# A fused QKV projection on one core: loads of x two pairs ahead issued in front of two pairs' stores, and two stores of the last pair on the other queue

## The chip, the core and the metric

The kernel runs on one core of a Trainium2 chip. TensorE (PE) multiplies, VectorE (DVE), ScalarE (ACT) and GpSimd (POOL) move and combine data, SyncE (SP) only issues DMAs. PE's weight loads have a row of their own, PEld. The metric is the device time of one execution, in microseconds (us). Three runs of the kernel before gave 360.57, 360.79 and 361.13 us; the median is 360.79 us.

## The reference

```python
def reference(x, w_qkv):               # x (16, 512, 768), w_qkv (768, 2304), float32
    qkv = np.matmul(x, w_qkv)
    q, k, v = qkv[..., :768], qkv[..., 768:1536], qkv[..., 1536:]
    return np.stack([q, k, v], axis=0).astype(np.float32)
```

x is 8192 rows of 768 numbers, 25 MB; the output is 8192 rows of 2304 numbers, 75 MB; the weights are 7 MB.

## The kernel before, in words

**Tiling.** The 8192 rows are worked on in 32 pairs of row blocks; a pair is 2 x 128 rows, numbered 0 to 31 in the code and in this document. (The fourth and fifth pairs are pairs 3 and 4.) The 2304 output columns are two blocks of 1024, called a (q = 0) and b (q = 1) here, and a remainder of 256 between them. "5a" is block a of pair 5.

**Seven products.** From pair 2 on, a pair times a block of 1024 columns is a 2 x 2 by 2 x 2 product computed with seven products in place of eight (a Strassen scheme). Each product is three matmuls of 128x128 by 128x512 that accumulate in one PSUM bank. Products 1 and 2 use bf16 copies of x (`xb`) and of the weights, products 3 to 7 use sums of quarters of x (`sr`, made by `sums_x` on POOL) and of the weights. `do(u, n)` (L269) issues product n of block u and the instructions that carry the bank into the output tile `u.o`: ACT writes a quarter of it (L267 for product 1, L286 for product 6, L292 for product 7, L296 for product 4), DVE adds a bank to a quarter (L293 after L292, L299 after product 3). `summed(a, b)` (L353) runs products 6, 6, 5, 7, 5, 7, 4, 3, 4, 3 of two blocks, 30 matmuls, and then stores each block. Several products share a bank: product 3 accumulates into the bank of product 5 after L293 has read it, product 7 into that of product 6 after L286 has read it.

**x.** `load_x(p, eng)` (L141) loads a pair as four DMAs of 192 KB into a tile `xin` (three buffers): two are issued by SP, two by the queue named. `transpose(p)` (L155) turns it on DVE into `xf`, whole or in two halves; `round_x` (L205) on POOL makes the bf16 copy, `sums_x` (L225 to L229) on POOL the sums.

**Stages.** Pairs 0 and 1 use ordinary bf16 products while the weights arrive. Block a of pair 2 is done among them; its block b (`u2`) is done together with pair 3. Then `two(a, b, early)` (L335) runs pair 3 and pair 4: products 1, the remainder (`rem`, L321), products 2, then `summed`. `early` is a function called in the middle: it transposes the next pair and issues loads. From pair 5 on a loop takes two pairs at a time (`summed` for one, then `plain`, then `summed` for the other); its first pass transposes the first half of pair 6 ahead of pair 5's `summed` and the second half within it. `last` (L412) does pair 31 and stores it in pieces.

**What sets the order.** The schedule is written by hand: each engine and each queue runs its instructions in the order in which the program gives them. SP issues every DMA of this part of the run, loads and stores, in one queue; from pair 9 on, half of every second pair's loads are issued by ACT. A store waits on SP until the last quarter of its half block is written, and everything behind it on SP waits too. Eight semaphores tell of DMAs' landings in turn, and an issue also waits until the DMA that last used its semaphore has landed, so at most eight are in flight.

**Buffers.** Output tiles `o` come from a pool of five and are taken in turn: 5a takes the one of block b of pair 1, 5b that of 3a, the blocks of pair 6 those of 3b and 4a, and 7a that of 4b. The first write to a tile waits until its former contents have been stored. `rem` has two output tiles `orem` of its own.

**Loads around the change.** Pair 5 is loaded in the first `early` (L624 to L626), within pair 3's `two`. In the second `early`, within pair 4's `two`, come the loads of pair 6; the loads of pair 7 come after that `two`:

```python
    def early():
        ahead(ND + 3, True)
        load_x(ND + 4, nc.sync)

    two(quad(ND + 2, 0), quad(ND + 2, 1), early)
    load_x(ND + 5, nc.sync)
    transpose(ND + 4, 2, 0)
```

ND is 2. So SP's order is: stores of `u2`, stores of pair 3 (L306, L307 for a, L310, L311 for b), loads of pair 6, the remainder's store of pair 4 (L331), stores of pair 4, loads of pair 7, loads of pair 8.

**The end.** In `last`, `store_cols` (L391) stores a quarter of a block: one DMA of 256 KB (L397), or two of 128 KB where the quarter crosses a border between two of the three outputs. In the last loop each block's quarter of product 4 is stored from ACT's queue and the quarter of product 3 from SP's; for block b the former is two DMAs. Behind them ACT copies the last remainder (L407) and stores it (L409).

Of the kernel before, what the change touches and what calls it, by code (L numbers as in the profile page):

```python
# [10 lines left out]
def kernel(  # L11
# [20 lines left out]
    nc = tc.nc  # L32
# [10 lines left out]
    CB = 512  # L43
# [81 lines left out]
    def load_x_half(p, h, eng):  # L125
        rows = x_flat[p * 2 * P:(p + 1) * 2 * P, :].rearrange("(g b) k -> b g k", b=G)
        for i in (2 * h, 2 * h + 1):
            eng.dma_start(xin[p][i * G:(i + 1) * G], rows[:, :, i * KC:(i + 1) * KC])
# [12 lines left out]
    def load_x(p, other):  # L141
        xin[p] = xin_pool.tile([P, 2 * P // G, KC], fp32, name="xin")
        load_x_half(p, 0, nc.sync)
        if other is not None:
            load_x_half(p, 1, other)

    def transpose(p, parts=1, which=None):
        if p not in xf:
            xf[p] = xf_pool.tile([P, KT, 2 * P], fp32, name="xf")
        turned = xf[p][:].rearrange("p j (g b) -> p g j b", b=G)  # L150
        rows = xin[p][:].rearrange("p g (a j) -> p g j a", a=G)
        n = 2 * P // G // parts
        for i in range(parts) if which is None else (which, ):
            g = i * n
            nc.vector.transpose(turned[:, g:g + n], rows[:, g:g + n])  # L155
# [84 lines left out]
    def quad(p, q, pool=o_pool, tag="o"):  # L240
        u = Quad()
        u.p, u.q = p, q
        u.o = pool.tile([P, 2, 2 * CB], fp32, name="o", tag=tag)
        u.x = u.y = u.z = None
        return u

    def product(u, n, ps, start):
        t1, t2, t3, t4 = ts[u.q]
        if n <= 2:
            h = (n - 1) * KH  # L250
            lhs = [xb[u.p][:, h + j, :P] for j in range(KH)]
            rhs = [b1[u.q][:, h + j, :] for j in range(KH)]
        else:
            k, t = {3: (4, b22[u.q][:]), 4: (0, t4), 5: (1, t1), 6: (2, t2), 7: (3, t3)}[n]
            lhs = [sr[u.p][:, k, j, :] for j in range(KH)]
            rhs = [t[:, j, :] for j in range(KH)]
        for j in range(KH):
            nc.tensor.matmul(  # L258
                ps[:], lhs[j], rhs[j],
                start=(start and j == 0), stop=(j == KH - 1), skip_group_check=True,  # L260
            )

    def bank():
        return ps_pool.tile([P, CB], fp32, name="ps")

    def evacuate(u):
        nc.scalar.activation(u.o[:, 0, :CB], u.x[:], ident)  # L267

    def do(u, n, out=True):  # L269
        c11, c12 = u.o[:, 0, :CB], u.o[:, 0, CB:]  # L270
        c21, c22 = u.o[:, 1, :CB], u.o[:, 1, CB:]
        if n == 1:
            u.x = bank()
            product(u, 1, u.x, True)
            if out:
                evacuate(u)
        elif n == 2:
            u.z = bank()
            product(u, 2, u.z, True)
            nc.vector.tensor_tensor(c11, c11, u.z[:], op=add)  # L280
        elif n == 6:
            first = u.x is None
            if first:
                u.x = bank()
            product(u, 6, u.x, first)
            nc.scalar.activation(c12, u.x[:], ident)  # L286
        elif n == 5:
            u.y = bank()
            product(u, 5, u.y, True)
        elif n == 7:  # L290
            product(u, 7, u.x, False)
            nc.scalar.activation(c22, u.x[:], ident)  # L292
            nc.vector.tensor_tensor(c22, c22, u.y[:], op=add)  # L293
        elif n == 4:
            product(u, 4, u.x, False)
            nc.scalar.activation(c21, u.x[:], ident)  # L296
        elif n == 3:
            product(u, 3, u.y, False)
            nc.vector.tensor_tensor(c12, c12, u.y[:], op=add)  # L299
# [4 lines left out]
    def store_quad(u):  # L304
        if u.q == 0:
            nc.sync.dma_start(rows_of(0, u.p, 0, H), u.o[:, :, :H])  # L306
            nc.sync.dma_start(rows_of(1, u.p, 0, 2 * CB - H), u.o[:, :, H:])  # L307
        else:
            part = 2 * H - Q_OFF[1]
            nc.sync.dma_start(rows_of(1, u.p, H - part, H), u.o[:, :, :part])  # L310
            nc.sync.dma_start(rows_of(2, u.p, 0, H), u.o[:, :, part:])  # L311
# [9 lines left out]
    def rem(p, eng=nc.sync, between=None):  # L321
        ps = ps_pool.tile([P, 2, REM], fp32, name="ps")
        rem_row(p, 0, ps[:, 0, :])
        if between is not None:
            between()
        rem_row(p, 1, ps[:, 1, :])

        def copied():
            o = or_pool.tile([P, 2, REM], fp32, name="orem")
            act.activation(o[:], ps[:], ident)  # L330
            return lambda: eng.dma_start(rows_of(1, p, R_OFF - H, R_OFF - H + REM), o[:])  # L331

        return copied

    def two(a, b, early, u=None):  # L335

        do(a, 1)
        do(b, 1, u is None)
        if u is None:
            early()  # L340
            rem(a.p)()()
        else:
            middle(u)
            copied = rem(a.p, between=lambda: third(u))
            evacuate(b)
            early()
            copied()()
            fourth(u)
        do(a, 2)
        do(b, 2)  # L350
        summed(a, b)

    def summed(a, b, between={}, store=True):  # L353

        for i, (u, n) in enumerate(
            ((a, 6), (b, 6), (a, 5), (a, 7), (b, 5), (b, 7), (a, 4), (a, 3), (b, 4), (b, 3))
        ):
            do(u, n)
            if n == 3 and store:
                store_quad(u)  # L360
            between.get(i, lambda: None)()
# [28 lines left out]
    def store_cols(u, r, lo, hi, eng):  # L390

        c = Q_OFF[u.q] + lo
        end = Q_OFF[u.q] + hi
        while c < end:
            n = min(end, (c // H + 1) * H)
            row = (2 * u.p + r) * P
            eng.dma_start(  # L397
                out_flat[c // H, row:row + P, c % H:c % H + n - c],
                u.o[:, r, c - Q_OFF[u.q]:n - Q_OFF[u.q]],
            )  # L400
            c = n

    def rem_stored(p, r):
        ps = bank()
        rem_row(p, r, ps[:, :REM])
        o = or_pool.tile([P, 2, REM], fp32, name="orem")
        nc.scalar.activation(o[:, 0, :], ps[:, :REM], ident)  # L407
        row = (2 * p + r) * P
        nc.scalar.dma_start(out_flat[1, row:row + P, R_OFF - H:R_OFF - H + REM], o[:, 0, :])  # L409

    def last(a, b):

        do(a, 1)
        do(b, 1)
        rem_stored(a.p, 0)
        for u in (a, b):
            do(u, 2)
            store_cols(u, 0, 0, CB, nc.sync)
        do(a, 6)
        do(b, 6)  # L420
        for u in (a, b):
            do(u, 5)
            do(u, 7)
            store_cols(u, 1, CB, 2 * CB, nc.sync)
        for u in (a, b):
            do(u, 4)
            store_cols(u, 1, 0, CB, nc.scalar)
            do(u, 3)
            store_cols(u, 0, CB, 2 * CB, nc.sync)
        rem_stored(a.p, 1)  # L430


    ND = 2
# [60 lines left out]
    def middle(u):  # L494
        do(u, 6)
        do(u, 5)
        act.activation(u.o[:, 1, CB:], u.y[:], ident)

    def third(u):
        c22 = u.o[:, 1, CB:]  # L500
        product(u, 7, u.x, False)
        dve.tensor_tensor(c22, c22, u.x[:], op=add)
        do(u, 3)

    def fourth(u):
        do(u, 4)
        store_quad(u)

    def ahead(p, reversed_pair):
        transpose(p)  # L510
        if reversed_pair:
            sums_x(p)
            round_x(p)
        else:
            round_x(p)
            sums_x(p)
# [46 lines left out]
    u = quad(2, 0)  # L563
# [59 lines left out]
    def early():  # L623
        ahead(ND + 2, False)  # L624
        load_x(ND + 3, nc.sync)

    two(quad(ND + 1, 0), quad(ND + 1, 1), early, u2)

    def early():
        ahead(ND + 3, True)  # L630
        load_x(ND + 4, nc.sync)

    two(quad(ND + 2, 0), quad(ND + 2, 1), early)
    load_x(ND + 5, nc.sync)
    transpose(ND + 4, 2, 0)

    for p in range(ND + 3, NP - 1, 2):
# [14 lines left out]
        a, b = quad(p, 0), quad(p, 1)  # L652
        summed(a, b, {5: turned} if first else {}, False)
        c, d = quad(p + 1, 0), quad(p + 1, 1)
        plain(a, b, c, d, early, lambda: rem(c.p)()())
        summed(c, d, {0: lambda: p + 3 < NP and transpose(p + 3, 2, 0)})
    last(quad(NP - 1, 0), quad(NP - 1, 1))


# [28 lines left out]
```

## Time and profile before

| | |
|---|---|
| median of three runs | 360.79 us |
| profiled execution | 360.87 us |
| its span | 359.1 us |
| PE busy | 352.8 us, 98% of the span |
| DVE busy | 262.9 us, 73% |
| ACT busy | 185.5 us, 52% |
| POOL busy | 177.6 us, 49% |
| DMA | 108.10 MB, 301 GB/s on average |

The profile is one execution, read on the core's engines. A row of the timeline has its start, its length in us, engine, line, operation, output<-inputs, and how often it came; in square brackets stands how long the engine was idle before it and what it was waiting for. "SPq" and "ACTq" are the queues' own instructions, such as the issue of a DMA. A row of the DMA view has the tiles, the issuing queue, the number of issues, the size of one and the median time from issue to landing. The chain of work that ended last follows the end of the run back from each step to what released it; its rows are start, length and what. Ends of matmuls are modelled.

### The profile page before, as it was taken

To read this page: it belongs to the slowest core of one execution; us is meant where nothing else is said; L and a number is where in the kernel's file an instruction comes from. 1 tells how busy PE (TensorE), PEld (TensorE's weight loads), DVE (VectorE), ACT (ScalarE), POOL (GpSimd) and SP (SyncE) were. 2 spreads that over 40 slices of the span, in tenths; PEclk is the share of its full clock that TensorE was granted. 3 is DMA by queue.
4 is the path that set the end of the run, shared out by engine and by line. 5 is a ranking of instruction groups with operands and counts; after the bars stand their busy time and mean duration, and the time that the engine had idled before them with its cause. 6 is when DMAs were issued, how large, how long until landed. Compare 5 with 4: busy or idle time off the path is not lost.

```text
span 359.1 us, 5325 instructions
## 1 busy us (share of the span) xinstructions
PE 352.8 (98%) x1776; PEld 252.3 (70%) x1776; DVE 262.9 (73%) x308; ACT 185.5 (52%) x317; POOL 177.6 (49%) x184
## 2 busy tenths in 40 slices
PE   8999999899999999999999999999999999999995
PEld 4474677668777686777868777686877768677674
DVE  3798876696776958778696876959777695877643
ACT  4587755445454554545545454553645545364553
POOL 0031783375666354665535566353665535566420
PEclk9999999999999999999999999999999999999999
DMA  7997999998999898997979899698999989896497
GB/s 298 378 347 236 322 381 382 373 256 328 310 308 348 231 377 208 342 287 241 379 201 381 237 319 325 197 406 216 349 266 306 330 218 373 222 339 235 170 358 263
DMA packets 81563, 108.10 MB, mean 301 GB/s; under 512 B 4992, under 2 KB 61568, under 8 KB 81536
## 3 DMA queue, kind: packets, MB, share of 16 engines
q1 hardware_dynamic: 74288, 102.25, 84.7%
q10 hardware_dynamic: 7248, 5.51, 5.7%
q8 instruction: 14, 0.23, 0.3%
q14 instruction: 13, 0.11, 0.1%
HBM read 32.24 MB, written 75.50 MB: 300 GB/s over the span
## 4 chain that ended last, share of the span: by engine, by line
PE 94%; DMA 3%; ACT 1%; DVE 0%; ACTq 0%; issue 0%; SPq 0%
PE ps L258 77%; PE ps L316 12%; PE ps L479 6%; DMA xin<-in_x_dram 2%; DMA out_dram<-o 2%; ACT xc L166 0%; PE ps L185 0%; ACTq L397 0%; DVE o L299 0%; DVE o L293 0%; ACT o L296 0%; SPq L162 0%; ACT orem L407 0%; SPq L306 0%; ACTq L407 0%
## 5 line engine op out<-in xcount | busy, mean ns | idle before, releaser
L258 PE MATMUL ps<-t,s 128*128 128x512 f32 x720 | 177.9, 395 | 0.0
L258 PEld LDWEIGHTS ps<-t,s 128*128 128x128 f32 x720 | 134.9, 188 | 29.6 <-ACT o L267 0.2
L155 DVE STREAM_TRANSPOSE xf<-xin 128x768 f32<-128x768 f32 (+1 forms) x45 | 93.4, 2077 | 5.6 <-DMA xin<-in_x_dram 5.5
L258 PE MATMUL ps<-b,xb 128*128 128x512 bf16 x360 | 85.4, 379 | 0.0
L293 DVE TENSOR_TENSOR o<-o,ps 128x512 f32<-128x512 f32 x58 | 39.7, 687 | 53.9 <-ACT o L292 53.9
L205 POOL CAST xb<-xf 128x1536 bf16<-128x1536 f32 x28 | 41.2, 1471 | 58.1 <-DVE xf L155 58.1
L225 POOL TENSOR_TENSOR s<-xf 128x384 fp32r<-128x384 f32 x29 | 29.5, 1017 | 72.6 <-DVE xf L155 72.6
L258 PEld LDWEIGHTS <-xb 128*128 128x128 bf16 x360 | 33.9, 98 | 36.8 <-issue 4.2
L292 ACT ACTIVATE o<-ps 128x512 f32<-128x512 f32 x58 | 34.7, 598 | 43.5 <-PE ps L258 43.5
L299 DVE TENSOR_TENSOR o<-o,ps 128x512 f32<-128x512 f32 x60 | 41.1, 687 | 20.0 <-PE ps L258 18.8
L258 PE MATMUL ps<-b,s 128*128 128x512 f32 x180 | 50.7, 390 | 1.1 <-DVE o L293 1.1
L296 ACT ACTIVATE o<-ps 128x512 f32<-128x512 f32 x60 | 35.9, 598 | 25.9 <-PE ps L258 23.4
L369 DVE TENSOR_TENSOR o<-o,ps 128x512 f32<-128x512 f32 x78 | 47.8, 682 | 0.0
L316 PE MATMUL ps<-w_rem,xb 128*128 128x256 bf16 x384 | 47.3, 273 | 0.0
L286 ACT ACTIVATE o<-ps 128x512 f32<-128x512 f32 x60 | 36.0, 601 | 19.5 <-PE ps L258 15.8
L316 PEld LDWEIGHTS <-xb 128*128 128x128 bf16 x384 | 37.2, 98 | 11.6 <-issue 0.8
L330 ACT ACTIVATE orem<-ps 128x512 f32<-128x512 f32 x31 | 18.5, 598 | 48.7 <-PE ps L316 33.4
L258 PEld LDWEIGHTS ps<-b,s 128*128 128x128 f32 x180 | 33.7, 188 | 8.5 <-issue 1.5
L226 POOL TENSOR_TENSOR s<-s,xf 128x384 fp32r<-128x384 f32 x29 | 29.6, 1020 | 2.3
L227 POOL TENSOR_TENSOR s<-xf 128x384 fp32r<-128x384 f32 x29 | 29.4, 1014 | 0.0
L229 POOL TENSOR_TENSOR s<-xf,s 128x384 fp32r<-128x384 f32 x29 | 29.3, 1009 | 0.0
L373 ACT ACTIVATE o<-ps 128x512 f32<-128x512 f32 x26 | 15.6, 599 | 17.4 <-PE ps L258 16.8
(46 smaller groups left out, 160.8 us busy)
## 6 DMA issues: line engine op xcount, KB each, us to landing
out_dram<-o SPq DMA_DIRECT2D x62, 768.0 KB, 4.6
xin<-in_x_dram SPq DMA_DIRECT2D x88, 192.0 KB, 5.6
out_dram<-o SPq DMA_DIRECT2D x65, 256.0 KB, 3.8
out_dram<-orem SPq DMA_DIRECT2D x31, 256.0 KB, 2.4
xin<-in_x_dram ACTq DMA_DIRECT2D x24, 192.0 KB, 4.3
st<-in_w_qkv_dram SPq DMA_DIRECT2D x5, 768.0 KB, 8.0
xin<-in_x_dram SPq DMA_DIRECT2D x2, 768.0 KB, 4.9
st<-in_w_qkv_dram SPq DMA_DIRECT2D x6, 256.0 KB, 6.0
```

Of the source, the lines that this page charges most:

```text
L155: nc.vector.transpose(turned[:, g:g + n], rows[:, g:g + n])
L205: nc.gpsimd.tensor_copy(out=xb[p][:], in_=xf[p][:])
L225: 1: lambda g: g.tensor_tensor(s[:, 1], a21, a22, op=add),
L226: 2: lambda g: g.tensor_tensor(s[:, 2], s[:, 1], a11, op=sub),
L258: nc.tensor.matmul(ps[:], lhs[j], rhs[j], start=(start and j == 0), stop=(j == KH - 1), skip_group_check=True,)
L286: nc.scalar.activation(c12, u.x[:], ident)
L292: nc.scalar.activation(c22, u.x[:], ident)
L293: nc.vector.tensor_tensor(c22, c22, u.y[:], op=add)
L296: nc.scalar.activation(c21, u.x[:], ident)
L299: nc.vector.tensor_tensor(c12, c12, u.y[:], op=add)
L316: nc.tensor.matmul(ps, xb[p][:, j, r * P:(r + 1) * P], w_rem[j // KH][:, j % KH, :], start=(j == 0), stop=(j == KT - 1), skip_group_check= ...
L369: dve.tensor_tensor(c, c, u.z[:], op=add)
```

## The change

The load of x of pair 6 moves out of the second `early` into the first `two` (the branch with `u2`, which runs only for pair 3), right behind `fourth(u)`, which stores `u2`; so it stands on SP ahead of the stores of pair 3. The load of pair 7 moves from behind the second `two` into its `early`; so it stands ahead of the remainder's store and of the stores of pair 4. In `last`, the quarter of product 4 of block b is stored from SP's queue, that of block a from ACT's as before.

```diff
@@ two
             early()
             copied()()
             fourth(u)
+            load_x(a.p + 3, nc.sync)
         do(a, 2)
         do(b, 2)
         summed(a, b)
@@ last
         for u in (a, b):
             do(u, 4)
-            store_cols(u, 1, 0, CB, nc.scalar)
+            store_cols(u, 1, 0, CB, nc.scalar if u is a else nc.sync)
             do(u, 3)
             store_cols(u, 0, CB, 2 * CB, nc.sync)
@@ pairs 3 and 4
     def early():
         ahead(ND + 3, True)
-        load_x(ND + 4, nc.sync)
+        load_x(ND + 5, nc.sync)
 
     two(quad(ND + 2, 0), quad(ND + 2, 1), early)
-    load_x(ND + 5, nc.sync)
     transpose(ND + 4, 2, 0)
```

The number and size of all DMAs and the orders of PE, DVE and POOL are the same before and after; SP issues two DMAs more and ACT two less.

## The prediction

> **What bounds the kernel now.** I read the page's shares first, then the chain of work that ended last, then the timeline around the one place where that chain leaves TensorE, and at last the landings of the DMAs there. The chain by engine, from the page:
>
> ```profile
> PE 94%; DMA 3%; ACT 1%; DVE 0%; ACTq 0%; issue 0%; SPq 0%
> ```
>
> The kernel is bound by TensorE: nearly all of its end is matmuls standing one behind the other. So an edit pays only where TensorE waits, or in the tail behind its last matmul. In order of time the chain leaves TensorE in mid-run once:
>
> ```profile
> 63.85 5.55 DMA out_dram<-o
> 69.45 0.66 DVE o L293
> ```
>
> The reader should not take the first row at its word: the L293 add behind it waits for old stores whose semaphores later DMAs share, and the profile names the last of these. The timeline of all engines shows what stood in front of L293. "T6.0" and "T6.1" below are the two half transposes of pair 6 (pairs count from 0), "5a" and "5b" the two blocks of pair 5:
>
> ```profile
> 62.22 0.84 PE L258 MATMUL ps<-b,s 128*128 128x512 f32 x3
> ...
> 62.90 0.84 PE L258 MATMUL ps<-t,s 128*128 128x512 f32 x3
> ...
> 64.26 4.92 PE L258 MATMUL ps<-t,s 128*128 128x512 f32 x21
> ...
> 64.46 0.69 DVE L299 TENSOR_TENSOR o<-o,ps 128x512 f32<-128x512 f32 x1 [0.67 <-PE ps L258]
> ...
> 65.19 1.28 ACT L286 ACTIVATE o<-ps 128x512 f32<-128x512 f32 x2 [0.81 <-PE ps L258]
> ...
> 67.18 0.60 ACT L292 ACTIVATE o<-ps 128x512 f32<-128x512 f32 x1 [0.71 <-PE ps L258]
> 67.94 1.59 DVE L155 STREAM_TRANSPOSE xf<-xin 128x768 f32<-128x768 f32 x1 [2.79 <-DMA xin<-in_x_dram]
> 68.54 0.60 ACT L292 ACTIVATE o<-ps 128x512 f32<-128x512 f32 x1 [0.76 <-PE ps L258]
> ...
> 69.45 1.25 DVE L293 TENSOR_TENSOR o<-o,ps 128x512 f32<-128x512 f32 x2
> ...
> 70.25 0.94 PE L258 MATMUL ps<-b,s 128*128 128x512 f32 x3 [1.07 <-DVE o L293]
> 70.61 1.63 DVE L155 STREAM_TRANSPOSE xf<-xin 128x768 f32<-128x768 f32 x1
> ...
> 72.38 1.47 POOL L205 CAST xb<-xf 128x1536 bf16<-128x1536 f32 x1 [6.68 <-DVE xf L155]
> ...
> 72.42 1.47 PE L258 MATMUL ps<-b,xb 128*128 128x512 bf16 x6
> ...
> 75.03 1.46 PE L258 MATMUL ps<-b,xb 128*128 128x512 bf16 x6
> ```
>
> VectorE ends L299 at 65.15, then stands 2.79 us at T6.0 because x of pair 6 has not landed; the two L293 adds, whose input was there at 67.78 (67.18 + 0.60), queue behind T6.0 until 69.45. Product 3 of 5a accumulates into the bank that the first L293 reads, so TensorE stops 1.07 us and resumes at 70.25. A late load of x is the only stop of TensorE here.
>
> **The change, step by step.** Edit one: the four DMAs that load x of pair 6 move ahead of the four stores of pair 3, and those of pair 7 ahead of those of pair 4. Nothing is added or removed; 4 loads and 4 stores trade places on SP's queue, twice. SP's issues before:
>
> ```profile
> 51.88 0.50 SPq L311 DMA_DIRECT2D out_dram<-o  x1
> ...
> 53.64 0.37 SPq L306 DMA_DIRECT2D out_dram<-o  x1
> ...
> 54.50 0.69 SPq L307 DMA_DIRECT2D out_dram<-o  x1
> ...
> 55.28 1.05 SPq L310 DMA_DIRECT2D out_dram<-o  x1
> ...
> 56.42 1.10 SPq L311 DMA_DIRECT2D out_dram<-o  x1
> ...
> 57.58 3.50 SPq L128 DMA_DIRECT2D xin<-in_x_dram  x4
> ```
>
> What matters is when the loads land. From narrow windows of the DMA view, the time from issue to landing of the stores issued at 51.88, 53.64, 54.50 and 56.42, then SP's row of the fourth load and its landing:
>
> ```profile
> out_dram<-o SPq DMA_DIRECT2D x1, 768.0 KB, 7.6
> ...
> out_dram<-o SPq DMA_DIRECT2D x1, 768.0 KB, 7.8
> ...
> out_dram<-o SPq DMA_DIRECT2D x1, 256.0 KB, 7.6
> ...
> out_dram<-o SPq DMA_DIRECT2D x1, 768.0 KB, 8.4
> ...
> 60.52 0.57 SPq L128 DMA_DIRECT2D xin<-in_x_dram  x1
> ...
> xin<-in_x_dram SPq DMA_DIRECT2D x1, 192.0 KB, 7.3
> ```
>
> Landings: 59.5, 61.4, 62.1, 64.8 and 67.8. They come in the order of issue and at steps that follow the bytes: 2.0 us for a 768 KB store, 0.7 for 256 KB, 3.0 for the four loads together (64.8 to 67.8). Between 51 and 68 the transfers are a line at a counter, some 7 us long, and a place in the line is a time. Estimate for after, from these steps: the loads of pair 6 take the issue slots from 53.64 on and land at 59.5 + 3.0 = 62.5; the stores of 3a follow at 62.5 + 2.0 + 0.7 = 65.2, those of 3b at 65.2 + 0.7 + 2.0 = 67.9, the loads of pair 7 at 70.9.
>
> T6.0 can then start as soon as L299 ends, at 65.19; its data, there since 62.5, has 2.7 us to spare. It ends at 66.8; the first L293 starts with its ACT input at 67.8 and ends at 68.5. TensorE's rate there is 0.68 us for three matmuls (62.22 to 62.90), 0.227 each, so after 21 of them it comes to product 3 of 5a at 64.26 + 4.77 = 69.03: 0.5 us after L293 is done. The second L293 (input 68.54 + 0.60 = 69.14) ends at 69.85; its product is due at 64.26 + 27 x 0.227 = 70.39, again 0.5 later. So no wait is left. The 30 matmuls of pair 5's ten products took 72.42 - 64.26 = 8.16 us and take 30 x 0.227 = 6.81: **minus 1.35 us**. That is the stop of 1.07 plus what the restart lost before and after it.
>
> What hid the moved stores, and is late next: the stores of 3a go from landing at 62.1 to 65.2. Their buffer goes to 5b, whose first write is the second L286, at 65.87 (65.19 + half of 1.28 and a little). Cover 0.7 us, and beyond it L286 may slip until TensorE needs its bank again for product 7 of 5b, at 64.26 + 15 x 0.227 = 67.67; less its 0.60 it may start as late as 67.0. Cost nothing; without cover, 1 us per us from a landing at 67.0 on. The stores of pair 4 come later likewise, behind the loads of pair 7; their buffers are wanted only by blocks of pairs 6 and 7. The remainder's store of pair 4 also falls behind, and nothing but a buffer two pairs on waits for it. ScalarE and POOL queue nothing behind any of these DMAs. The loads of pair 5 stand ahead of everything moved. Bounds of edit one: above, no gain, if the loads land as before; below, 1.35, since TensorE has no other stop there.
>
> Edit two: in the last pair, two 128 KB stores of the second block go from ScalarE's queue to SP's. The end before, SP's, TensorE's and ScalarE's rows of the timeline, then from narrow windows the landings of the last 256 KB store on SP, of the remainder's store on ScalarE, of an earlier 128 KB store that met an empty queue, and of a 256 KB one on ScalarE's queue:
>
> ```profile
> 353.97 0.85 SPq L397 DMA_DIRECT2D out_dram<-o  x2
> ...
> 354.42 0.83 PE L316 MATMUL ps<-w_rem,xb 128*128 128x256 bf16 x6
> ...
> 354.56 0.86 ACTq L397 DMA_DIRECT2D out_dram<-o  x2
> ...
> 355.33 0.33 SPq L397 DMA_DIRECT2D out_dram<-o  x1
> ...
> 355.52 0.38 ACT L407 ACTIVATE orem<-ps 128x256 f32<-128x256 f32 x1 [0.99 <-PE ps L316]
> 355.94 0.34 ACTq L409 DMA_DIRECT2D out_dram<-orem  x1
> ...
> out_dram<-o SPq DMA_DIRECT2D x1, 256.0 KB, 2.6
> ...
> out_dram<-orem ACTq DMA_DIRECT2D x1, 128.0 KB, 2.3
> ...
> out_dram<-o SPq DMA_DIRECT2D x1, 128.0 KB, 1.7
> ...
> out_dram<-o ACTq DMA_DIRECT2D x1, 256.0 KB, 2.8
> ```
>
> Before, the last landing is the remainder's, 355.94 + 2.3 = 358.2; SP's 256 KB store lands at 355.33 + 2.6 = 357.9. After, ScalarE is free of 0.86 us of issuing, but TensorE ends the remainder only at 354.42 + 0.83 = 355.25, so L407 moves from 355.52 to 355.29, its store to 355.71 and its landing to 358.0, 0.2 earlier. SP is busy until 354.82 with the two stores of 353.97, issues the two moved ones until about 355.72, and only then the 256 KB store: 355.76 instead of 355.33, landing at 355.76 + 2.6 = 358.36. The last landing moves from 358.24 to 358.36: I take **plus 0.1**, by the rows of the same place. Ends: with 2.8, 358.6, plus 0.4; with 1.7 for the moved pair's second store (355.3 + 1.7 = 357.0) and 0.7 for 256 KB behind it, 357.7, but the remainder's store then still has to land by 2.0, at 357.7: minus 0.5.
>
> The Trainium skill, "DMA: Bandwidth & Descriptors", section "Issuing engines are not separate DMA queues", says that DMAs from all queues share the same engines and that a second queue saves only the issuer's time; by that rule the edit would give what it saves on ScalarE, minus 0.2 in place of plus 0.1, if SP had that time to spare. The rows say that SP has not.
>
> Sum: 1.35 less, 0.1 more: minus 1.25 us. The profiled execution took 360.87 us (span 359.1), which gives 359.6; the median of the runs is 0.08 lower, so **359.5 us**.
>
> **Rivals.** B, VectorE paces it: T6.1 stands behind the second L293, which waits for ScalarE until 69.14, so T6.1 starts at 69.85, only 0.76 earlier than 70.61, while TensorE runs 1.35 earlier. POOL's cast at 72.38 then ends at 71.6 + 1.5 = 73.1, and the first product that reads it, in the group at 75.03, is due at 73.7. Margin 0.6 us where there was 1.2. If that is overdrawn, the gain is VectorE's 0.76 and no more: 360.79 - 0.76 + 0.1 = 360.1, up to 360.4 if POOL loses another 0.3. Against it: two other waits would have to grow by half a microsecond.
>
> C, the load is not earlier: if the loads do not land earlier for being issued earlier, T6.0 starts as before and only edit two is left: 360.9. Against it, all six landings above come in order of issue.
>
> D, slower: 3a's stores land too late for 5b. From 65.87 + 1.2 = 67.0 on TensorE waits one for one, from 67.0 + 1.35 = 68.4 on the kernel is slower than before. With the longest time to landing shown, 8.4 us, from an issue at 58.3 (the slot after 57.58 for the second store of 3a) it is 66.7, still inside; it takes 10 us. At a landing of 69.0 the time would be 360.79 - 1.35 + 2.0 + 0.1 = 361.5. For it: the line at the counter is full, and a load moved up pushes 3.0 us onto every store behind it.
>
> **How the numbers follow.** The forecast A, 359.5, holds 0.76, with its own range from 360.79 - 1.35 - 0.5 = 358.9 to 359.9 (edit two at plus 0.4). B 0.10, C 0.05, D 0.09. The range 358.9 to 360.4 takes in A and B and leaves out C and D, 0.14. About 0.2%, 0.7 us, is what a measurement of this kernel can tell from no change; under 360.1 is faster: A and a quarter of B, 0.79. Within: most of B and C, 0.12. Slower: D, 0.09.
>
> **What would show it.** T6.0 starting near 65.2 with no wait for x; no idle time of TensorE before product 3 of 5a, near 69.0; the group of 72.42 at about 71.1; every later row of the chain 1.35 earlier, in steps of the same length. L286 of 5b at 65.9 or a few tenths later with a store as releaser would show the thin cover of D. At the end, the last landing would be SP's 256 KB store, not the remainder's, and the distance from TensorE's last matmul to the end of the span would grow by 0.1. The prediction is wrong if TensorE idles anywhere between 62 and 80, or if the loads of pair 6 land after 66.

## The result, and the profile after

The changed kernel takes 359.66 us (median of 12 runs, 359.51 to 360.18), beside it the kernel before 360.81 us (12 runs, 360.04 to 361.54). The ratio is 0.9969, with a 95% interval of 0.9960 to 0.9978: about 1.1 us faster, between 0.8 and 1.4. The profiled execution took 359.82 us with a span of 358.0 us; that of before took 360.87 us.

The same stretch of the timeline after, all engines, the rows that answer to those of before. This execution runs 0.30 us later than the other from before the change on (product 3 of pair 4's first block begins at 62.52, there at 62.22), so 0.30 has to be taken off when times are compared:

```profile
62.52 0.84 PE L258 MATMUL ps<-b,s 128*128 128x512 f32 x3
...
64.56 4.92 PE L258 MATMUL ps<-t,s 128*128 128x512 f32 x21
64.76 0.69 DVE L299 TENSOR_TENSOR o<-o,ps 128x512 f32<-128x512 f32 x1 [0.68 <-PE ps L258]
...
65.36 1.64 DVE L155 STREAM_TRANSPOSE xf<-xin 128x768 f32<-128x768 f32 x1
65.49 1.28 ACT L286 ACTIVATE o<-ps 128x512 f32<-128x512 f32 x2 [0.81 <-PE ps L258]
...
68.11 0.69 DVE L293 TENSOR_TENSOR o<-o,ps 128x512 f32<-128x512 f32 x1 [1.10 <-ACT o L292]
...
69.32 0.84 PE L258 MATMUL ps<-b,s 128*128 128x512 f32 x3
...
70.07 1.59 DVE L155 STREAM_TRANSPOSE xf<-xin 128x768 f32<-128x768 f32 x1
...
71.80 1.47 POOL L205 CAST xb<-xf 128x1536 bf16<-128x1536 f32 x1 [6.33 <-DVE xf L155]
```

T6.0 has no bracket: it starts as L299 ends, 65.36, and waits for no load. L293 now waits for its own input from ScalarE and is done at 68.80, half a microsecond before product 3 of 5a needs its bank at 69.32, which has no bracket either. With 0.30 taken off, that product begins at 69.02 where it began at 70.25.

The landings of the fourth load of pair 6 and of the second store of 3a, SP's row and its time to landing:

```profile
56.08 0.47 SPq L128 DMA_DIRECT2D xin<-in_x_dram  x1
...
xin<-in_x_dram SPq DMA_DIRECT2D x1, 192.0 KB, 5.6
...
57.11 0.45 SPq L307 DMA_DIRECT2D out_dram<-o  x1
...
out_dram<-o SPq DMA_DIRECT2D x1, 256.0 KB, 7.3
```

The load is there at 61.7 and the store at 64.4. The second L286, which overwrites that buffer, comes at about 66.2 and is not held.

At the end of the run, TensorE's last matmuls, the last store on each queue and the times to landing of SP's and of ScalarE's:

```profile
353.36 0.83 PE L316 MATMUL ps<-w_rem,xb 128*128 128x256 bf16 x6
...
354.85 0.41 SPq L398 DMA_DIRECT2D out_dram<-o  x1
...
354.64 0.34 ACTq L410 DMA_DIRECT2D out_dram<-orem  x1
...
out_dram<-o SPq DMA_DIRECT2D x1, 256.0 KB, 2.3
...
out_dram<-orem ACTq DMA_DIRECT2D x1, 128.0 KB, 1.9
```

The last matmul ends at 354.19, the last landing is SP's, at 357.2: 3.0 us behind it. Before it was the remainder's, at 355.94 + 2.3 = 358.2, also 3.0 us behind a last matmul that ended at 355.25. The end's edit changed who is last, and not when.

### The profile page after: what moved, and what is told of

Same layout as the page of the kernel before. It is cut to its first block, busy times and chain, and to the rows that moved or that the text cites. A ratio compares the mean times of both kernels' runs of the same rounds, so it can differ in the third digit from the quotient of the medians.

```text
span 358.0 us, 5305 instructions
## 1 busy us (share of the span) xinstructions
PE 351.3 (98%) x1757; PEld 252.6 (71%) x1776; DVE 263.6 (74%) x308; ACT 185.3 (52%) x317; POOL 177.6 (50%) x184
## 4 chain that ended last, share of the span: by engine, by line
PE 70%; POOL 15%; DVE 6%; DMA 4%; issue 3%; SPq 1%; ACT 0%; DVEq 0%
PE ps L258 56%; PE ps L316 11%; DVE xf L155 6%; POOL xb L205 5%; POOL s L226 3%; POOL s L225 3%; POOL s L227 3%; PE ps L480 3%; DMA xin<-in_x_dram 2%; DMA st<-in_w_qkv_dram 2%; SPq L137 1%; SPq L92 0%; SPq L162 0%; ACT xb L214 0%; DVE o L299 0%
## 5 line engine op out<-in xcount | busy, mean ns | idle before, releaser
L258 PE MATMUL ps<-b,xb 128*128 128x512 bf16 x343 | 81.6, 379 | 1.4 <-ACT xb L214 0.3
L293 DVE TENSOR_TENSOR o<-o,ps 128x512 f32<-128x512 f32 x58 | 39.9, 688 | 55.7 <-ACT o L292 55.7
L225 POOL TENSOR_TENSOR s<-xf 128x384 fp32r<-128x384 f32 x29 | 31.0, 1069 | 72.0 <-DVE xf L155 70.3
L299 DVE TENSOR_TENSOR o<-o,ps 128x512 f32<-128x512 f32 x60 | 41.1, 687 | 20.0 <-PE ps L258 18.8
L286 ACT ACTIVATE o<-ps 128x512 f32<-128x512 f32 x60 | 36.0, 601 | 19.4 <-PE ps L258 15.7
L227 POOL TENSOR_TENSOR s<-xf 128x384 fp32r<-128x384 f32 x29 | 29.5, 1016 | 0.0
```

The source lines that it names most:

```text
L225: 1: lambda g: g.tensor_tensor(s[:, 1], a21, a22, op=add),
L227: 3: lambda g: g.tensor_tensor(s[:, 3], a11, a21, op=sub),
L258: nc.tensor.matmul(ps[:], lhs[j], rhs[j], start=(start and j == 0), stop=(j == KH - 1), skip_group_check=True,)
```

## The experiments

The theory: the load of pair 6 came so late that T6.0 stood in VectorE's queue in front of L293, and that was the whole difference (theory L). The rivals: the earlier load of pair 7 or the end's edit carries part of it (S), and, against the change, the stores that were pushed back cost something of their own (D). Ratios are to the kernel before in the same set of runs on the same chip; its medians were 360.42, 360.49 and 360.51 us in the three sets.

| kernel | median us | ratio to before | 95% interval |
|---|---|---|---|
| load of pair 6 alone | 359.69 | 0.9980 | 0.9970 to 0.9989 |
| the same, again | 359.84 | 0.9985 | 0.9973 to 0.9997 |
| load of pair 7 alone | 361.08 | 1.0016 | 1.0007 to 1.0025 |
| the end's edit alone | 360.54 | 1.0001 | 0.9990 to 1.0013 |
| both loads | 359.42 | 0.9972 | 0.9961 to 0.9983 |
| the same, again | 359.32 | 0.9962 | 0.9950 to 0.9974 |
| the changed kernel, again | 359.49 | 0.9965 | 0.9952 to 0.9977 |
| T6.0 behind L293 | 360.14 | 0.9993 | 0.9984 to 1.0003 |
| both loads ahead of pair 3's stores | 360.93 | 1.0017 | 1.0000 to 1.0033 |
| one store of 1 MB more | 361.45 | 1.0029 | 1.0017 to 1.0041 |
| two stores of 1 MB more | 366.60 | 1.0171 | 1.0152 to 1.0191 |
| the last pair's two stores split over the queues | 359.41 | 0.9973 | 0.9964 to 0.9982 |

### The parts one by one

Load of pair 6 alone: of the diff only `load_x(a.p + 3, nc.sync)` behind `fourth(u)`; `early` loads nothing and the load of pair 7 stays behind `two`.

> Only the load of pair 6 is moved in front of pair 3's stores; the load of pair 7 and the end stay as before. Theory L (the late load of pair 6 in front of the two L293 is the whole of it): 1.3 us faster than before, 359.4 to 359.6 us, TensorE with no idle time before product 3 of 5a, T6.0 starting with L299's end. Rival S (the earlier load of pair 7 or the end carries part of it): at least 0.4 us of the gain is missing, 359.9 or more. In T6.1 to T7 the profile should read as in the changed kernel.

Load of pair 7 alone:

```diff
     def early():
         ahead(ND + 3, True)
         load_x(ND + 4, nc.sync)
+        load_x(ND + 5, nc.sync)
 
     two(quad(ND + 2, 0), quad(ND + 2, 1), early)
-    load_x(ND + 5, nc.sync)
```

> Only the load of pair 7 is moved, in front of the remainder's store and the stores of pair 4, behind the load of pair 6 which stays where it was. Theory L: no change, 360.6 to 361.0 us, T6.0 waits 2.5 to 3 us for x and TensorE 1.0 to 1.2 us for L293 as before; T7 had its x in time before. Rival S: 0.4 us or more faster. Slower only if the stores of pair 4, some 3 us later in line, hold a block of pair 6.

The end's edit alone is the diff's line in `last` and nothing else.

> Only the two 128 KB stores of the last pair's block b go to SP's queue. Prediction on record: plus 0.1 us (ends minus 0.5 and plus 0.4), the last landing being SP's 256 KB store. From the changed kernel's profile, where the last landing stands as far behind the last matmul as before: 0.0, 360.7 to 360.9 us. Rival (the shorter queue of ScalarE ends the run): minus 0.2.

Both loads is the diff without that line.

> Both loads moved, the end as before. Theory L: the whole gain, 359.4 to 359.7 us, not to be told from the changed kernel. Rival (the end's edit gives 0.2 or more): 359.9.

The end's edit can't be told from nothing by the times (1.0001, with an interval that leaves 0.4 us either way), and both loads without it give what the changed kernel gives. The load of pair 6 alone takes the stop away in its profile; nothing of TensorE waits from 50 us on. But T7, the transpose of pair 7, now waits for x; VectorE's row in that kernel:

```profile
76.96 3.00 DVE L155 STREAM_TRANSPOSE xf<-xin 128x1536 f32<-128x1536 f32 x1 [0.67 <-DMA xin<-in_x_dram]
```

The next load in the row is the next to be late, once TensorE runs ahead. Its median came out 0.27 us above both loads. The pair was run again, with the changed kernel beside it:

> Only the load of pair 6 moved, once more: no stop of TensorE, so the same as both loads within 0.2 us, though T7 waits 0.7 us for x in its profile. If that wait reaches TensorE in some executions (rival S), the median stands 0.2 to 0.5 us above both loads, as in the first pair of runs (0.27).

> Both loads moved, the end as before, once more: the same as the changed kernel beside it within 0.2 us (the end's edit is worth nothing). If the end's edit is worth something either way, the medians differ by more than that with the same sign as in the earlier pair of runs (0.24 below).

> The changed kernel itself, side by side with its parts on one chip: 0.8 to 1.3 us below the kernel before, whose own times scatter with the length of the stop (0.4 and 1.1 us in two profiles of it with and without the end's edit); its own scatter under 0.7 us.

The difference is there again, 359.84 against 359.32 and 359.49, though the intervals of the ratios overlap in both sets. It is in the scatter: 359.17 to 360.86 for the load of pair 6 alone, 359.18 to 359.72 and 359.39 to 359.51 for the others. Its profile, of an execution of 359.28 us, has T7 waiting 0.88 us and TensorE stopping nowhere. So S is likely right by some tenths, and not shown: the earlier load of pair 7 keeps T7 covered. That T7's wait reaches TensorE in those executions of that kernel that took over 360 us is argued from this; none of them was profiled.

The load of pair 7 alone is slower by 0.16%, which neither theory had. The waits of TensorE, then VectorE's T6.0 and SP's row of the fourth load of pair 6 with its landing, all of that kernel:

```profile
PE ps L258 <- DVE o L293: 1.6, 1, 1.6
...
68.35 1.57 DVE L155 STREAM_TRANSPOSE xf<-xin 128x768 f32<-128x768 f32 x1 [3.36 <-DMA xin<-in_x_dram]
...
59.88 0.54 SPq L128 DMA_DIRECT2D xin<-in_x_dram  x1
...
xin<-in_x_dram SPq DMA_DIRECT2D x1, 192.0 KB, 8.3
```

The stop is the same one, 1.6 us long instead of 1.1. The last load of pair 6 was issued at 59.88, before at 60.52, and yet landed later, at 68.2 instead of 67.8: with four more loads right behind it, it took longer. In the two other profiles that leave both loads where they were it landed earlier still, at 67.1 (the end's edit alone) and 66.8 (T6.0 behind L293, below), so 68.2 is the latest of four. Moving pair 7's load pays only together with pair 6's.

### The stop without any DMA moved

T6.0 goes behind the two L293 on VectorE; all loads stay where they were:

```diff
-    transpose(ND + 4, 2, 0)
...
         def turned():
+            if p == ND + 3:
+                transpose(p + 1, 2, 0)
             transpose(p + 1, 2, 1)
```

> The loads stay as before; T6.0 is put behind the two L293 of pair 5 on VectorE, directly before T6.1. If the queueing of L293 behind T6.0 on VectorE is what stops TensorE (theory L), the stop before product 3 of 5a is gone though x lands no earlier. But T6.0 and T6.1 then run from 69.85 to 73.1, POOL's cast from 73.2 to 74.6, and the first product that reads it is due at 73.7: TensorE waits 0.9 there instead of 1.35 earlier, 360.3 to 360.5 us. Rival (TensorE's stop comes from a store or from ScalarE, with L293 late for another reason): a stop of about 1.1 us before product 3 of 5a stays, and the cast's delay comes on top: 361.5 or more.

The timeline of that kernel, SP's row of the fourth load of pair 6 and its landing, the matmuls of product 3 of 5a, both half transposes, the cast and the first product that reads it:

```profile
60.11 0.52 SPq L128 DMA_DIRECT2D xin<-in_x_dram  x1
...
xin<-in_x_dram SPq DMA_DIRECT2D x1, 192.0 KB, 6.7
...
68.82 0.84 PE L258 MATMUL ps<-b,s 128*128 128x512 f32 x3
...
69.57 3.02 DVE L155 STREAM_TRANSPOSE xf<-xin 128x768 f32<-128x768 f32 x2
...
72.72 1.47 POOL L205 CAST xb<-xf 128x1536 bf16<-128x1536 f32 x1 [7.58 <-DVE xf L155]
...
74.25 1.47 PE L258 MATMUL ps<-b,xb 128*128 128x512 bf16 x6 [0.60 <-POOL xb L205]
```

The stop before product 3 is gone though no load was moved. The load happened to land at 66.8 in this execution, against 67.8 in the profile before (this one runs 0.20 ahead). Even so it would have stopped TensorE from its old place: by the steps of the profile before, T6.0 would start at 66.9, L293 at 68.4 and product 3 at 69.2, an estimate of 0.4 us too late. So it was the queueing behind T6.0. In its place TensorE stops 0.60 us for the cast, where I expected 0.9. That is the margin that rival B turned on. The net, 0.9993, can't be told from no change; the median is 0.35 us lower.

### How much the moved stores can bear

Three kernels push the stores of 3a further back than the change does. First the load of pair 7 too goes in front of them:

```diff
             load_x(a.p + 3, nc.sync)
+            load_x(a.p + 4, nc.sync)
```

(and is taken out of `early`).

> The changed kernel with the load of pair 7 moved further, directly behind the load of pair 6 and so also in front of pair 3's stores. The stores of 3a land 2.2 to 3.0 us later than in the changed kernel (64.4), at 66.5 to 67.4. Rival D's threshold (5b's first write may start as late as 67.3 in that profile's time): L286 of 5b waits 0.6 to 1.5 us for the store, TensorE 0 to 0.1 us; time as the changed kernel, 359.5 to 359.8 us. If the cover is thinner than I think: 360.2 or more.

Then a store of the second block of pair 2, of 1 MB, is made once or twice more behind the load of pair 6, `store_quad(u)`; the output stays the same.

> The changed kernel with block b of pair 2 stored twice more (the same numbers to the same place, 2 x 1 MB) behind the load of pair 6, so that the line of transfers in front of pair 3's stores is 5.3 us longer. Theory of the line: the stores of 3a land at about 69.7, L286 of 5b waits for them until then, TensorE stops for 69.7 - 67.3 = 2.4 us, 361.5 to 362.5 us, slower than before by rival D's mechanism. Rival (the engines have room, or the stores of 3a pass those in front of them): no stop at 5b, 359.5 to 360.

> The changed kernel with block b of pair 2 stored once more (1 MB, the same numbers to the same place) behind the load of pair 6: a dose between the changed kernel (second store of 3a landed at 64.4, no stop) and two stores more (70.4, a stop of 3.3 us). By rival D's threshold, 5b's first write may start as late as 66.9 to 67.3 without a stop: the store should land at about 67 and TensorE stop 0 to 0.4 us; 359.5 to 360.0 us. If each us of delay costs from the first on: 2.5 us slower than the changed kernel, 362.

SP's row of the second store of 3a, its landing, and the second L286 behind it, for the load of pair 7 in front:

```profile
61.38 0.40 SPq L307 DMA_DIRECT2D out_dram<-o  x1
...
out_dram<-o SPq DMA_DIRECT2D x1, 256.0 KB, 6.9
...
68.47 0.60 ACT L286 ACTIVATE o<-ps 128x512 f32<-128x512 f32 x1 [2.99 <-DMA out_dram<-o]
...
PE ps L258 <- ACT o L286: 1.6, 1, 1.6
```

The store lands at 68.3, not at 66.5 to 67.4 as I expected: I had taken 2.1 us for four loads from the changed kernel, where stores follow them, and eight loads one behind the other took 2.95 us per four. L286 waits 2.99 us for it, TensorE 1.6, and the kernel takes 360.93 us where I expected 359.5 to 359.8. For one store of 1 MB more, L286's row, then the next pass's first half transpose of pair 8, the issue and landing of the load that it needs, and TensorE's stop:

```profile
66.50 0.60 ACT L286 ACTIVATE o<-ps 128x512 f32<-128x512 f32 x1 [0.51 <-DMA out_dram<-o]
...
82.43 1.62 DVE L155 STREAM_TRANSPOSE xf<-xin 128x768 f32<-128x768 f32 x1 [2.07 <-POOL s L227]
...
76.44 0.31 SPq L128 DMA_DIRECT2D xin<-in_x_dram  x1
...
xin<-in_x_dram SPq DMA_DIRECT2D x1, 192.0 KB, 5.9
...
84.78 0.93 PE L258 MATMUL ps<-b,s 128*128 128x512 f32 x3 [0.76 <-DVE o L293]
```

Here the cover of 3a holds: L286 waits 0.51 us for the store and TensorE not at all. So between a landing at 66.4 (no stop) and one at 68.3 (1.6 us) lies the threshold, where the prediction had 67.0. But the kernel is slower all the same, 361.45 us and 1.0029, where I expected at most 360.0. The line that was lengthened stays long: the last load of pair 8 lands at 76.44 + 5.9 = 82.3, its transpose starts at 82.43 (the profile names POOL, but the landing is what came just before), L293 queues behind it, and TensorE stops 0.76 us. It is the stop of the kernel before, one pass later. The profiled execution took 360.96 us, half a microsecond less than the median; whether that stop is longer in the others was not profiled.

With two stores more TensorE's waits and the windows in which it stopped and went on (us, busy times with counts, then TensorE's granted clock, DMA share and GB/s):

```profile
PE ps L258 <- ACT o L286: 3.3, 1, 3.3
...
68.00:72.00 4.00, 0.76 (x3) 0.67 (x4) 0.29 (x1) 1.09 (x2) 0.00 (x0) 0.98 1.05 360
72.00:76.00 4.00, 4.00 (x12) 3.09 (x12) 3.15 (x4) 1.31 (x3) 0.64 (x1) 0.59 1.07 259
76.00:80.00 4.00, 4.00 (x26) 2.38 (x25) 3.43 (x6) 1.20 (x3) 3.92 (x5) 1.00 1.05 397
```

The stop is 3.3 us, and then the granted clock is 0.59 for the next 4 us; a second stop of 0.7 us follows at 89.8. In the timeline of that kernel:

```profile
71.24 2.42 PE L258 MATMUL ps<-t,s 128*128 128x512 f32 x6 [3.27 <-ACT o L286]
...
73.46 1.48 PE L258 MATMUL ps<-b,s 128*128 128x512 f32 x3
...
74.74 1.11 PE L258 MATMUL ps<-t,s 128*128 128x512 f32 x3
75.69 0.84 PE L258 MATMUL ps<-b,s 128*128 128x512 f32 x3
```

Three matmuls take 1.28 us (73.46 to 74.74) where they take 0.68 at full clock, and the twelve from 71.24 to 75.69 take 4.45 us for 2.72: 1.7 us lost on top of the stop. 3.3, 1.7 and 0.7 make 5.7 of the 6.2 us by which this profiled execution (366.04 us) is behind that of the changed kernel. I had expected a stop of 2.4 us and at most 362.5 us: the second store of 3a landed at 70.4 and not at 69.7, and neither the clock nor the second stop was in the sum.

### What sets the tail

One of the two 128 KB stores of block b goes on each queue:

```diff
-            store_cols(u, 1, 0, CB, nc.scalar if u is a else nc.sync)
+            if u is a:
+                store_cols(u, 1, 0, CB, nc.scalar)
+            else:
+                store_cols(u, 1, 0, CB // 2, nc.scalar)
+                store_cols(u, 1, CB // 2, CB, nc.sync)
```

> The changed kernel with the last pair's two 128 KB stores of block b one on each queue, so that SP issues its last 256 KB store about 0.5 us earlier and ScalarE's remainder is not held. If the tail is set by the issue of the last store and its time to landing: 0.2 to 0.4 us faster than the changed kernel, 359.2 to 359.5 us, last landing 2.6 to 2.8 us behind the end of the last matmul instead of 2.98. If it is set by the bytes still to be moved, landing in line at 0.33 us per 128 KB: the same as the changed kernel within 0.1 us.

TensorE's last matmuls, ScalarE's last store and its landing in that kernel, then its DMA share and rate in the window behind the last matmul:

```profile
353.02 0.83 PE L316 MATMUL ps<-w_rem,xb 128*128 128x256 bf16 x6
...
354.31 0.34 ACTq L410 DMA_DIRECT2D out_dram<-orem  x1
...
out_dram<-orem ACTq DMA_DIRECT2D x1, 128.0 KB, 2.5
...
354.00:356.00 2.00, 0.00 (x0) 0.00 (x0) 0.00 (x0) 0.27 (x1) 0.00 (x0) 1.00 1.08 389
```

The last landing is at 356.8, 3.0 us behind the last matmul's end at 353.85, as in the other two arrangements. The store that comes last changes, and its time to landing with it (1.9 us for the remainder's in the changed kernel, 2.5 here), but three orders of the same bytes end alike, with the DMA engines full at 389 GB/s in the window. In all fourteen profiles the distance is 2.97 to 3.01 us. That is what a tail set by the bytes still to be moved would do; no run moved fewer of them.

## Why the prediction was right

**What bounds the kernel, and the stop.** Right. T6.0 starts with L299's end, L293 with its own input, TensorE has no idle time before product 3 of 5a, and that product begins at 69.02 by the clock of the profile before, where 69.03 was worked out. The 1.35 us of the step is what the two profiles show up to the end: the last matmuls begin at 354.42 and 353.36, 1.06 apart, and the second execution had started 0.30 behind. Moving T6.0 alone shows that the queue on VectorE was the mechanism, not the load as such. Two slips in the reading change nothing: the input of the second L293 was there at 69.14 and not at 67.78, and the landings that were read from the line are five, not six. The size of the step has some luck in it: the sum took the stop of one profiled execution, 1.07 us, and the profile of the end's edit alone has 0.38 at the same place (see below). The medians of both loads moved, with and without the end's edit, are 1.0 to 1.2 us below those of the kernel before.

**The line of transfers.** Right in order and in time: the loads of pair 6 were to land at 62.5 and the stores of 3a at 65.2. In this profile they landed at 61.7 and 64.4, the four loads taking 2.1 us and not 3.0; in the six others in which the loads of pair 6 alone stand in front of those stores they landed at 60.6 to 62.9 and at 63.3 to 65.4.

**The cover of the moved stores and rival D.** The threshold at 67.0 and the price, one for one behind it, held. On the clock of the profile before (by the start of product 3 of pair 4's first block, 62.22 there) the second store of 3a landed at 66.2 with one store more, without a stop; at 68.6 with pair 7's load in front, with a stop of 1.6 us; and at 70.3 with two stores more, with a stop of 3.3. The second of these is slower than before by 0.17%, behind the break-even that was put at 68.4. Behind a stop of some 3 us the price was too low: the clock was missing from it.

**Edit two.** Plus 0.1 predicted, 0.0 measured. The term that was mis-sized is SP's last store: its issue came 0.15 later than worked out (354.85, against 355.76 less 1.06), but it took 2.3 us to land and not 2.6, which fits a time to landing that is a place in the line and not a property of the store. The 128 KB store of 1.7 us, issued at 351.88, had not met an empty queue: the three stores issued before it were still in flight and landed at 352.4 to 353.1. Only the end of minus 0.5 rests on it.

**Rival B.** Its place was right: with both half transposes late, POOL's cast is what stops TensorE. In the changed kernel the cast ends at 73.27 and the product that reads it begins at 73.98: the margin was 0.7 us where 0.6 was worked out.

**What was left out of the sum.** A part for the load of pair 7: it was costed at nothing, and T7 had its x in time before, by 0.1 us (the last load of pair 7 landed at 76.8, T7 began at 76.90). With TensorE 1.35 us earlier it would not have had; T7 waits 0.7 to 0.9 us when that load stays behind. How much of that reaches TensorE is open. The cover of an operation has to be read after the gain is taken off it.

The sum was 1.25 us and 359.5 us; the measured difference is 1.1 us (0.8 to 1.4) and the median 359.66 us.

## What to carry to other kernels

Where one engine is busy throughout, look for the one row where it has a bracket, and then for what stands in front of the releaser in its own queue: here it was a transpose waiting for a load, not the add that the matmul needed. When the transfers in flight form a line of several microseconds, as on SP's queue here, where the DMAs landed in the order of issue in every profile, moving a load up is a trade against the stores behind it; read the slack of each of these from who overwrites their buffers, and read it again with the gain taken off. At the end of a run in which the DMA engines are full, look first at the bytes left: here shuffling stores between queues changed which was last and not when.

## What the runs showed that was not expected

**The stop's length is not fixed.** It is 1.07 us in the profile before and 0.38 in that of the end's edit alone, which has the same program up to the last pair:

```profile
PE ps L258 <- DVE o L293: 0.4, 1, 0.4
...
67.22 1.61 DVE L155 STREAM_TRANSPOSE xf<-xin 128x768 f32<-128x768 f32 x1 [2.08 <-DMA xin<-in_x_dram]
```

There x is awaited for 2.08 us, before for 2.79. The times of the kernel before scatter accordingly, 359.34 to 361.54 us over all sets, those of the changed kernel less, 359.39 to 360.18, and those with T6.0 behind L293 less too, 360.01 to 360.62. Part of what the change does is to take a variable wait off the path. Why the same loads land at different times from one execution to the next is open.

**Loads behind loads land later.** The four loads of pair 6 took 2.1 to 3.0 us of the line in the twelve profiles in which stores follow them, and 3.2 and 3.6 us in the two in which four more loads do; in one of these, the load of pair 7 alone, the stop was 1.6 us long. What in the transfer is shared was not tried.

**A stop of 3.3 us costs 5.** After it the granted clock was 0.59 in the following 4 us; after the stops of 1.1 and 1.6 us it was 1.00. The Trainium skill, "TensorE: Matmul & The Clock Gate", section "What's actually happening", has the clock halved after an idle window of about 3.4 us. The matmuls at 0.43 us in place of 0.23 agree with the halving; the stop that brought it was a little shorter here, 3.27 us.
